# A delta-rule layer's forward substitution moved from GpSimd to VectorE, with the inverses' scratch in its two tiles

## The chip, the cores and the metric

The kernel runs on one core of one Trainium2 chip. The metric is the device time of one execution in microseconds (us). One core has five engines with an instruction queue each: TensorE (PE in the profile; its weight loads are PEld), VectorE (DVE), ScalarE (ACT), GpSimd (POOL) and SyncE (SP), which here issues most transfers between HBM and the on-chip buffer SBUF. Each engine works through its own list in order; an instruction that needs another engine's or a transfer's result waits for a semaphore, and everything behind it on its engine waits with it.

## What is computed

The reference is a decoder trunk of four pre-norm residual layers over 256 tokens and 1024 channels: a pooling mixer, a gated delta-rule mixer, a latent-attention mixer, and a pooling mixer again. The change touches only the second layer. Its core, cut to what matters, is:

```python
L = where(strict, einsum('bhnid,bhnjd->bhnij', k_beta, k) * decay, 0)
A = eye(C) + L                       # C = 64 tokens a chunk, 8 heads, 4 chunks
sol = triangular_solve(A, concat([v_beta, k_beta * exp(g)]), lower=True)
```

So a lower triangular matrix with ones on its diagonal has to be inverted for each head and chunk. The kernel takes the 256 tokens as two tiles of 128, one matrix of 128x128 for each tile and head (16 in all), in place of chunks of 64.

## The kernel before

All products of activations with weights run in three passes on TensorE: a float32 weight block is split into a high part (`whi`, ScalarE, L117) and a rest (`wlo`, L119, mostly on VectorE, in named cases on GpSimd), and `mm3` (L126 to L129) or `rows` (L167) adds up the three partial products. `weights` (L104 to L124) loads 512 KB from HBM on SyncE's queue into a tile `raw`, then makes the two parts of each 128x512 block. A block feeds 12 matmuls of 256 columns or 6 of 512 columns, so TensorE needs a fresh `wlo` from VectorE about every 1.4 us. The tiles `raw`, `whi`, `wlo` go round in rings.

The delta-rule layer (`gdn_layer`) runs through this list: `g0 k0 d a0 g1 k1 a1 s q0 v0 i v1 v2 q1 g2 u0 v3 u1 g3`. Here g are gate projections, k keys, q queries, v values (each a projection of 512 columns, for k, q and v followed by a short convolution on VectorE, L636, and a SiLU on ScalarE, L777 for values), a the lower triangles `LT`, d the decays, s the substitution, i the inverses, u first products with the inverses. The list is only the order in which the program is traced. The order in which each engine meets its instructions is set afterwards by a scheduler, which plays the program through with assumed durations and gives each engine what is ready first; so an edit in one place can shift rows of every engine near it. `issue_after` (the helper `later`) adds an order on one engine only: what is traced inside it comes behind the named instruction if that stands on the same engine.

The part that is changed works as follows.

- `substitution` (L713 to L744). The four 32x32 blocks on the diagonal of each of the 16 matrices, 64 blocks in all, are brought through HBM into a tile `Lb` with one block on each of 64 partitions (eight transfers `d_l<-LT`, L718, and one `Lb<-d_l`, L721). `Tb`, in the same layout, begins as 64 unit matrices. For r = 0 to 30 one instruction multiplies column r of the block with row r of the inverse so far, as an outer product of 31-r rows and r+1 columns, into `pr` (L726), and a second subtracts it from the rows of `Tb` below (L730). These 62 instructions depend on each other one by one. Then `Tb` goes to HBM (`d_t<-Tb`, L733) and comes back in eight transfers into the tiles `T` (L737). All of L726 and L730 runs on GpSimd.
- `mark["blocks"]` is the last of those instructions. The GpSimd work of `queries` (L758 to L763, with the power at L657) is put behind it.
- `inverses` (L788 to L840). VectorE transposes `T` into `U` (L800); TensorE multiplies `T` with `LT` (L809), VectorE masks the result into a scratch tile `X1` (L811), of which GpSimd has set one part to zero (L799), TensorE goes on with `X1` and `U` (L815), VectorE subtracts (L818), and a second round (L823 to L836) joins blocks of 64 to the full inverse. This is done for each of the two token tiles.

## Time and profile before

| quantity | value |
|---|---|
| runs of the kernel before | 859.46 us median of 3 (859.01 to 860.44) |
| the profiled execution, its own time | 857.47 us |
| its span in the trace | 855.8 us |
| mean granted TensorE clock | 0.991 |
| TensorE busy | 835.1 us, 98% of the span |
| VectorE busy | 594.5 us, 69% |
| ScalarE busy | 489.7 us, 57% |
| GpSimd busy | 153.7 us, 18% |

The profiled execution is one run; its time is 1.7 us longer than its span, and 2.0 us under the median of the timed runs. In the profile a row of a group gives the line, engine and operation, the tile written and the tiles read, the shape, how many there were, busy time and mean length, and the idle time ahead of them with what ended it. A row of a timeline gives the start, the length of the merged piece, and in brackets the idle time before it. Instructions that follow each other on one engine overlap a little in these rows: the next one starts before the last one's length is over. A row of the windows view gives, for each stretch, the busy time and count on each engine, the granted TensorE clock as a share of full speed, the share of the DMA engines in use and the GB/s moved. Line numbers are those of the kernel before.

### The profile page before, as it was taken

To read this page: it belongs to the slowest core of one execution; us is meant where nothing else is said; L and a number is where in the kernel's file an instruction comes from. 1 tells how busy PE (TensorE), PEld (TensorE's weight loads), DVE (VectorE), ACT (ScalarE), POOL (GpSimd) and SP (SyncE) were. 2 spreads that over 40 slices of the span, in tenths; PEclk is the share of its full clock that TensorE was granted. 3 is DMA by queue.
4 is the path that set the end of the run, shared out by engine and by line. 5 is a ranking of instruction groups with operands and counts; after the bars stand their busy time and mean duration, and the time that the engine had idled before them with its cause. 6 is when DMAs were issued, how large, how long until landed. Compare 5 with 4: busy or idle time off the path is not lost.

```text
span 855.8 us, 16129 instructions
## 1 busy us (share of the span) xinstructions
PE 835.1 (98%) x5967; PEld 777.7 (91%) x5967; DVE 594.5 (69%) x1140; ACT 489.7 (57%) x1007; POOL 153.7 (18%) x290
## 2 busy tenths in 40 slices
PE   7999999999999979999999999999999999999996
PEld 6999998988999969888979998999989989999986
DVE  4579876566988967556567659778767568766852
ACT  5565655467845635555465654566555576555642
POOL 5000000234227952032202002000000210000012
PEclk9999999999999989999999999999999999999998
DMA  6756656646655552222557676743652547666551
GB/s 201 250 177 194 179 191 210 184 148 203 191 146 156 169 172 90 85 74 99 172 154 215 204 157 174 195 137 93 171 167 75 173 151 217 178 192 182 194 195 51
DMA packets 111288, 140.43 MB, mean 164 GB/s; under 512 B 23340, under 2 KB 53224, under 8 KB 111208
## 3 DMA queue, kind: packets, MB, share of 16 engines
q1 hardware_dynamic: 109056, 138.17, 53.7%
q0 software_dynamic: 320, 1.06, 0.4%
q8 instruction: 47, 0.77, 0.4%
q10 hardware_dynamic: 1832, 0.16, 0.2%
q14 instruction: 33, 0.27, 0.1%
HBM read 137.79 MB, written 1.58 MB: 163 GB/s over the span
## 4 chain that ended last, share of the span: by engine, by line
PE 86%; DVE 4%; POOL 3%; issue 2%; DMA 2%; ACT 1%; SPq 1%; POOLq 0%; ACTq 0%
PE acc L167 34%; PE acc L128 12%; PE acc L127 12%; PE acc L129 12%; PE aux L127 2%; PE aux L128 2%; PE aux L129 2%; DVE vc L636 1%; DVE wlo L119 1%; DMA raw<-in_pool_w_in_dram 1%; PE aux L688 1%; DVE h L303 1%; PE aux L809 1%; PE tp L1168 1%; ACT junk L209 1%
## 5 line engine op out<-in xcount | busy, mean ns | idle before, releaser
L119 DVE TENSOR_TENSOR wlo<-raw,whi 128x512 fp32r<-128x512 f32 (+1 forms) x493 | 343.3, 719 | 161.9 <-ACT whi L117 159.9
L117 ACT CAST whi<-raw 128x512 fp32r<-128x512 f32 (+1 forms) x508 | 302.0, 619 | 263.1 <-PE acc L167 90.0
L128 PE MATMUL acc<-hTl,whi 128*128 128x256 f32 x832 | 235.5, 283 | 0.0
L127 PE MATMUL acc<-hTh,whi 128*128 128x256 f32 x832 | 234.5, 282 | 0.0
L129 PE MATMUL acc<-hTh,wlo 128*128 128x256 f32 x832 | 234.4, 282 | 0.0
L128 PEld LDWEIGHTS acc<-hTl,whi 128*128 128x128 f32 x832 | 157.3, 189 | 0.5
L127 PEld LDWEIGHTS acc<-hTh,whi 128*128 128x128 f32 x832 | 157.2, 189 | 0.5
L129 PEld LDWEIGHTS acc<-hTh,wlo 128*128 128x128 f32 x832 | 157.2, 189 | 0.2
L167 PE MATMUL acc<-whi,yTh 128*128 128x256 f32 (+1 forms) x384 | 116.2, 323 | 0.0
L167 PE MATMUL acc<-wlo,yTh 128*128 128x256 f32 (+1 forms) x384 | 116.2, 319 | 0.0
L167 PE MATMUL acc<-whi,yTl 128*128 128x256 f32 (+1 forms) x384 | 92.4, 321 | 0.0
L167 PEld LDWEIGHTS acc<-wlo,yTh 128*128 128x128 f32 x384 | 72.0, 188 | 5.1
L167 PEld LDWEIGHTS acc<-whi,yTh 128*128 128x128 f32 x384 | 71.8, 188 | 5.2
L167 PEld LDWEIGHTS acc<-whi,yTl 128*128 128x128 f32 x384 | 63.0, 188 | 5.6
L291 POOL TENSOR_TENSOR hg<-x,gain 128x256 f32<-128x256 f32 x18 | 15.3, 858 | 258.2 <-DVE x L353 255.5
L167 PE MATMUL acc<-whi,hTh 128*128 128x512 f32 (+1 forms) x144 | 55.8, 395 | 1.1 <-ACT hTh L195 1.0
L167 PE MATMUL acc<-wlo,hTh 128*128 128x512 f32 (+1 forms) x144 | 56.2, 396 | 0.4 <-DVE wlo L119 0.2
L167 PE MATMUL acc<-whi,hTl 128*128 128x512 f32 (+1 forms) x144 | 45.8, 390 | 0.0
L434 POOL COPY win<-u 128x4 f32<-128x4 f32 x8 | 2.8, 355 | 178.1 <-ACT u L428 178.1
L167 PEld LDWEIGHTS acc<-whi,hTh 128*128 128x128 f32 x144 | 27.4, 190 | 7.8 <-ACT hTh L195 2.2
L167 PEld LDWEIGHTS acc<-wlo,hTh 128*128 128x128 f32 x144 | 27.5, 191 | 6.8 <-DVE wlo L119 1.7
L167 PEld LDWEIGHTS acc<-whi,hTl 128*128 128x128 f32 x144 | 26.9, 190 | 5.8 <-DVE hTl L200 0.4
(337 smaller groups left out, 1437.0 us busy)
## 6 DMA issues: line engine op xcount, KB each, us to landing
raw<-in_pool_w_in_dram SPq DMA_DIRECT2D x60, 512.0 KB, 4.4
raw<-in_gdn_w_in_dram SPq DMA_DIRECT2D x48, 512.0 KB, 4.1
raw<-in_pool_w_out_dram SPq DMA_DIRECT2D x32, 512.0 KB, 4.4
raw<-in_mla_w_in_dram SPq DMA_DIRECT2D x24, 512.0 KB, 4.2
raw<-in_mla_w_uq_dram SPq DMA_DIRECT2D x36, 256.0 KB, 3.8
raw<-in_pool_w_grp_dram SPq DMA_DIRECT2D x16, 512.0 KB, 3.9
raw<-in_gdn_w_out_dram SPq DMA_DIRECT2D x16, 512.0 KB, 3.6
raw<-in_mla_w_ukv_dram SPq DMA_DIRECT2D x32, 256.0 KB, 3.4
```

The source lines that it names most:

```text
L117: a = nc.scalar.copy(hi, v)
L119: b = e.tensor_tensor(out=lo, in0=v, in1=hi.bitcast(F32), op=ALU.subtract)
L127: nc.tensor.matmul(o, lhsT=lhs[0], rhs=rhs[0], start=start, stop=False)
L128: nc.tensor.matmul(o, lhsT=lhs[0], rhs=rhs[1], start=False, stop=False)
L129: nc.tensor.matmul(o, lhsT=lhs[1], rhs=rhs[0], start=False, stop=stop)
L167: nc.tensor.matmul(o, lhsT=act(k, t * P, P)[x], rhs=parts[j][z][:, sl], start=k == first and x == z == 0, stop=k == last and x == 1)
L209: nc.scalar.activation(junk[:, :n], src, AF.Square, scale=scale, accum_out=o)
L291: nc.gpsimd.tensor_tensor(out=self.early[t, a], in0=xs[t][:, sl], in1=self.g[:, sl], op=ALU.mult)
L303: nc.vector.scalar_tensor_tensor(out=h[:, cut:], in0=xs[t][:, sl], scalar=r[:, 0:1], in1=self.g[:, sl], op0=ALU.mult, op1=ALU.mult)
L636: nc.vector.scalar_tensor_tensor(out=o[:, d:], in0=ps[:, :S - d], scalar=tp(3 - d, c), in1=o[:, d:], op0=ALU.mult, op1=ALU.add)
L688: nc.tensor.matmul(ps[:, b], lhsT=kT[hf][:, b, tt], rhs=rhs[hf][:, b, tt], start=True, stop=True)
L809: nc.tensor.matmul(ps[:, h], lhsT=LT[t][:, h], rhs=blocks(T[t], 0)[:, h], start=True, stop=True)
```

## The change

The two instructions of the substitution's loop are issued on VectorE in place of GpSimd. The scratch tiles `X1` of the inverses are no longer allocated; the full-height tiles that hold `Lb` and `Tb` are kept in a list, and `X1[0]` and `X1[1]` are views of them (32x32 elements a partition seen as 8x128). `Lb` and `Tb` themselves are, as before, the first 64 partitions. Nothing of the arithmetic changes.

```diff
-        Tb = big("Tb", B, B)[:M * Q]
+        Tb_ = big("Tb", B, B)
+        Tb = Tb_[:M * Q]
+        free = []
         nc.gpsimd.memset(Tb, 0.0)
         nc.gpsimd.memset(Tb.rearrange("m r c -> m (r c)")[:, ::B + 1], 1.0)
...
-            Lb = big("Lb", B, B)[:M * Q]
+            Lb_ = big("Lb", B, B)
+            Lb = Lb_[:M * Q]
+            free.extend((Lb_, Tb_))
             nc.sync.dma_start(out=Lb, in_=d_l.rearrange("m (r c) -> m r c", r=B))
             pr = small("pr", 256, bufs=1)[:M * Q]
             for r in range(B - 1):
                 n, c = B - 1 - r, r + 1
                 pv = pr[:, :n * c].rearrange("m (a b) -> m a b", a=n)
-                nc.gpsimd.tensor_tensor(out=pv, op=ALU.mult,
+                nc.vector.tensor_tensor(out=pv, op=ALU.mult,
                                         in0=Lb[:, r, r + 1:, None].to_broadcast([M * Q, n, c]),
                                         in1=Tb[:, r:r + 1, :c].to_broadcast([M * Q, n, c]))
                 tv = Tb[:, r + 1:, :c]
-                mark["blocks"] = nc.gpsimd.tensor_tensor(out=tv, in0=tv, in1=pv,
+                mark["blocks"] = nc.vector.tensor_tensor(out=tv, in0=tv, in1=pv,
                                                          op=ALU.subtract).ins
...
             U.extend(big("U", H, P) for _ in range(NT))
-            X1 = [big("X1", H, P) for _ in range(NT)]
+
+            X1 = [a.rearrange("p (h a) c -> p h (a c)", h=H) for a in free]
             for t in range(NT):
                 nc.gpsimd.memset(X1[t][:, :, 32:64], 0.0)
```

The edit moves line numbers by 2 to 5: the substitution's pair L726 and L730 becomes L730 and L734, `T` with `LT` L809 becomes L814, the transposes of the values L781 become L785, the scratch's zeros L799 become L804.

The scheduler's order of the engines changes with it. On VectorE, at the place where the substitution's input has landed, before (the projections' `wlo`, the query's `attnT`, the values' convolution `vc`):

```order
L119 TENSOR_TENSOR wlo<-raw,whi 128x512 x2
L679 TENSOR_REDUCE ssq<-sq 128x2x2
L119 TENSOR_TENSOR wlo<-raw,whi 128x512
L692 SCALAR_TENSOR_TENSOR attnT<-aux,rk,DT 128x128 x7
L679 TENSOR_REDUCE ssq<-sq 128x2x2
L692 SCALAR_TENSOR_TENSOR attnT<-aux,rk,DT 128x128
L636 SCALAR_TENSOR_TENSOR vc<-acc,tap,vc 128x255 x2
L119 TENSOR_TENSOR wlo<-raw,whi 128x512 x2
```

And now at the same place:

```order
L119 TENSOR_TENSOR wlo<-raw,whi 128x512
L730 TENSOR_TENSOR pr<-Lb,Tb 64x31
L734 TENSOR_TENSOR Tb<-Tb,pr 64x31
L730 TENSOR_TENSOR pr<-Lb,Tb 64x60
L734 TENSOR_TENSOR Tb<-Tb,pr 64x30x2
L730 TENSOR_TENSOR pr<-Lb,Tb 64x87
L681 TENSOR_REDUCE ssq<-sq 128x2x2
L734 TENSOR_TENSOR Tb<-Tb,pr 64x29x3
L730 TENSOR_TENSOR pr<-Lb,Tb 64x112
L694 SCALAR_TENSOR_TENSOR attnT<-aux,rk,DT 128x128 x2
```

From here to the last subtraction the 62 instructions of the substitution lie on VectorE among 82 others: 30 of L119, 42 of the convolution L636, 8 of `attnT` and 2 reductions. 25 of the 62 are followed directly by the next of the substitution, 37 by something else.

On TensorE, at the first product that reads `T`, before (numbers tell the tiles of a ring apart; `acc_4263` and `acc_4264` are the two banks of the last value projection, v3):

```order
L127 MATMUL acc_4263<-hTh0_2258,whi_4272 128x256
L128 MATMUL acc_4263<-hTl0_2259,whi_4272 128x256
L129 MATMUL acc_4263<-hTh0_2258,wlo_4271 128x256
L127 MATMUL acc_4263<-hTh0_2258,whi_4272 128x256
L809 MATMUL aux_3509<-T_2517,LT_2531 128x64 x8
L128 MATMUL acc_4263<-hTl0_2259,whi_4272 128x256
L129 MATMUL acc_4263<-hTh0_2258,wlo_4271 128x256
```

And now (the same projection's banks are `acc_4261` and `acc_4262`, its last block is `wlo_4371`):

```order
L127 MATMUL acc_4261<-hTh1_2267,whi_4372 128x256
L128 MATMUL acc_4261<-hTl1_2268,whi_4372 128x256
L129 MATMUL acc_4261<-hTh1_2267,wlo_4371 128x256
L814 MATMUL aux_3507<-T_2517,LT_2531 128x64 x8
L785 MATMUL tp_3931<-ident_101,vc_3921 128x128 x4
L785 MATMUL tp_3948<-ident_101,vc_3938 128x128 x4
L820 MATMUL aux_3517<-U_3501,Lb_3045 96x64 x8
L814 MATMUL aux_3527<-T_2518,LT_2532 128x64 x8
L677 MATMUL tp_4118<-ident_101,kqT_4093 128x128 x4
L127 MATMUL acc_4262<-hTh0_2258,whi_4266 128x256
```

The product has moved down. Between the last query product `attnT` of q0 and the first product with `T`, TensorE had 275 matmuls of 256 columns and 48 of 512 columns before, and now has 314 and 48; the transposes between them (L781, now L785) are 16 in both.

On GpSimd the 62 instructions are gone, the work of `queries` (L758 to L763) for the first four heads moves ahead of the place where the substitution ends, since its order behind `mark["blocks"]` binds only one engine, and the two memsets of the scratch (L799, now L804) come behind it, for they now wait until `Lb` and `Tb` have been read for the last time. On SyncE 18 weight loads instead of 15 stand between `Lb<-d_l` and `d_t<-Tb`, and none stands between `d_t<-Tb` and `T<-d_t`.

## The prediction

> **What bounds the kernel now.** I read the first part of the page, then TensorE's waits in the delta-rule layer (200 to 420 us), then the chain of waits and the windows around the longest of them.
>
> ```profile
> PE 835.1 (98%) x5967; PEld 777.7 (91%) x5967; DVE 594.5 (69%) x1140; ACT 489.7 (57%) x1007; POOL 153.7 (18%) x290
> ```
>
> ```profile
> PE aux L809 <- DMA T<-d_t: 6.1, 1, 6.1
> PE tp L675 <- ACT kqT L669: 0.9, 1, 0.9
> PE tp L781 <- ACT vc L777: 0.8, 1, 0.8
> ```
>
> TensorE is busy for 98% of the span, so the time ends where TensorE's work ends, and it moves only by what TensorE waits or is slowed. Its one long wait in this layer is for `T`, the result of the substitution. The chain of waits shows what that wait consists of (start, length, what):
>
> ```profile
> 306.45 0.59 POOL Tb L730
> ...
> 307.06 2.93 DMA d_t<-Tb
> ...
> 310.93 1.95 DMA T<-d_t
> ...
> 313.01 3.65 PE aux L809 x16
> ...
> 322.40 1.79 PE aux L809 x16
> ```
>
> The last subtraction ends at 307.06, and the way through HBM takes 5.95 us more until L809 starts at 313.01. The same 16 matmuls take 3.65 us there and 1.79 us for the second tile. The windows say why, and how full VectorE is meanwhile (columns: sum, PE, PEld, DVE, ACT, POOL, granted clock, DMA share, GB/s):
>
> ```profile
> 260.00:270.00 10.00, 10.00 (x87) 10.00 (x86) 8.41 (x21) 6.11 (x13) 8.70 (x17) 1.00 0.41 133
> 270.00:280.00 10.00, 9.22 (x77) 8.82 (x77) 10.00 (x20) 6.15 (x12) 9.14 (x12) 1.00 0.55 160
> 280.00:290.00 10.00, 10.00 (x87) 9.97 (x87) 10.00 (x18) 7.24 (x16) 9.21 (x13) 1.00 0.58 159
> 290.00:300.00 10.00, 9.93 (x58) 8.35 (x57) 8.41 (x15) 4.78 (x10) 9.22 (x13) 1.00 0.54 159
> 300.00:310.00 10.00, 6.88 (x38) 5.71 (x36) 6.95 (x10) 3.43 (x6) 9.13 (x15) 1.00 0.51 138
> ...
> 312.00:313.00 1.00, 0.00 (x0) 0.02 (x1) 0.00 (x0) 0.81 (x2) 0.00 (x0) 0.50 0.41 66
> 318.00:319.00 1.00, 1.00 (x9) 1.00 (x8) 0.21 (x2) 0.62 (x1) 0.00 (x0) 0.75 0.71 219
> ```
>
> After the wait the granted clock is 0.50 until some way into 318. That costs 3.65 - 1.79 = 1.9 us on L809 and, by the nine matmuls after it that follow at 0.21 instead of 0.12 us in the chain, about 0.9 more: 2.8 us. And VectorE, not GpSimd alone, is nearly full just here: 43.8 of the 50 us from 260 to 310. That is the engine the work moves to.
>
> **What the move takes off VectorE.** The splits `wlo` of VectorE are longer while GpSimd computes; first the groups from 100 to 250 us, then from 255 to 308:
>
> ```profile
> L119 DVE TENSOR_TENSOR wlo<-raw,whi 128x512 fp32r<-128x512 f32 x86 | 59.5, 713 | 30.4 <-ACT whi L117 30.0 <-PE acc L128 0.2
> ```
>
> ```profile
> L119 DVE TENSOR_TENSOR wlo<-raw,whi 128x512 fp32r<-128x512 f32 x29 | 27.2, 949 | 7.6 <-ACT whi L117 7.6
> ```
>
> So 29 x (0.949 - 0.713) = 6.8 us of VectorE's time there is waiting behind GpSimd, and it goes. GpSimd keeps these in the stretch (its groups, 255 to 312; in the new order they come ahead of the substitution's end):
>
> ```profile
> L119 POOL TENSOR_TENSOR wlo<-raw,whi 128x512 fp32r<-128x512 f32 x2 | 2.6, 1292 | 0.0
> L657 POOL TENSOR_TENSOR rq<-rq,halves 128x8 f32<-128x8 f32 x1 | 2.0, 1968 | 0.1
> L758 POOL TENSOR_TENSOR Gb<-Gb,kqT 128x512 f32<-128x512 f32 x1 | 1.3, 1257 | 0.0
> L759 POOL TENSOR_SCALAR rq<-ssq 128x8 f32<-128x8 f32 x1 | 0.5, 526 | 0.1
> ```
>
> That is 6.4 us of GpSimd. Before, 6.8 us of delay came with some 45 us of it, 0.15 us per us; the substitution's own instructions, which also read two tiles from SBUF, can now be delayed too, so I take 1.0 us (bounds 0 and 6.4). The Trainium skill, page "SBUF — State Buffer", section "SBUF: two separate sides", is stricter: GpSimd and a VectorE instruction with two SBUF inputs share one port pair, and whoever comes second waits for the other's whole instruction. The rows agree that only `wlo` suffers, and the convolution, which has one input in PSUM, does not. By that rule at its full strength the term would be 6.4 us in place of 1.0.
>
> **What it puts on VectorE.** No row shows the two instructions on VectorE. The nearest are tensor_tensor on SBUF tiles at both ends of their size (31 to 256 elements a partition), then one pair in which the second needs the first:
>
> ```profile
> L439 DVE TENSOR_TENSOR win<-win,corr 128x60 f32<-128x60 f32 x2 | 0.4, 208 | 0.0
> L435 DVE TENSOR_TENSOR win<-u 128x1020 f32<-128x1020 f32 x8 | 9.7, 1217 | 1.0 <-ACT u L428 1.0
> L967 DVE SCALAR_TENSOR_TENSOR rr<-kf,rr 128x64 f32<-128x64 f32 x4 | 0.9, 220 | 0.0
> ```
>
> ```profile
> 83.15 0.48 DVE L967 SCALAR_TENSOR_TENSOR rr<-kf,rr 128x64 f32<-128x64 f32 x2
> ```
>
> From 60 to 1020 elements the length grows by 1.051 ns an element, from a base of 208 - 60 x 1.051 = 145 ns. Each of the two instructions handles (31-r)(r+1) elements at step r, 5,456 over the 31 steps. So the 62 are 62 x 0.145 + 10,912 x 0.001051 = 20.5 us long. The pair takes 0.48 where each is 0.22, so a dependent successor costs 0.04 us on top. An independent one overlaps: in the timeline rows below, two L119 of 0.68 take 1.29, so one takes 0.61 of the engine's time. In the new order 25 of the 62 are followed by their own successor and 37 by something else, which at 0.08 us overlap gives 20.5 + 25 x 0.04 - 37 x 0.08 = 18.5 us. All overlapped it would be 15.5, none 23.0; the order decides for 18.5.
>
> What lies among them is priced by these rows of VectorE's timeline:
>
> ```profile
> 258.05 1.29 DVE L119 TENSOR_TENSOR wlo<-raw,whi 128x512 fp32r<-128x512 f32 x2 [2.35 <-ACT whi L117]
> 262.48 1.89 DVE L692 SCALAR_TENSOR_TENSOR attnT<-aux,rk,DT 128x128 f32<-128x128 f32 x7
> 264.30 0.68 DVE L679 TENSOR_REDUCE ssq<-sq 128x4 f32<-128x512 f32 x1
> 264.89 0.34 DVE L692 SCALAR_TENSOR_TENSOR attnT<-aux,rk,DT 128x128 f32<-128x128 f32 x1
> 290.76 2.03 DVE L636 SCALAR_TENSOR_TENSOR vc<-acc,tap,vc 128x253 f32<-128x253 f32 x5
> ```
>
> 30 splits at 0.61 are 18.3 us; 42 of the convolution at (2.03 - 0.47)/4 = 0.39, where 0.47 is one alone, 16.4; 8 `attnT` at (1.89 - 0.34)/6 = 0.26, 2.1; 2 reductions at 264.89 - 264.30 = 0.59, 1.2. Together 38.0 us. The windows bound it from below: 43.8 us busy from 260 to 310, less the 6.8, are 37.0.
>
> **The sum.** The substitution starts when `Lb` lands, which doesn't move; on GpSimd that was here:
>
> ```profile
> 259.39 0.23 POOL L726 TENSOR_TENSOR pr<-Lb,Tb 64x31 f32<-64x31 f32 x1 [13.50 <-DMA Lb<-d_l]
> ```
>
> On VectorE it then ends at 259.4 + 38.0 + 18.5 + 1.0 = 316.9, if VectorE waits for nothing else. ScalarE's `whi` and the weight loads, for which it waited 7.6 us before, are now ahead, since VectorE is the slow one. The way through HBM is unchanged, 5.95 us, so `T` reaches TensorE at 322.85 instead of 313.01: 9.8 us later. Against this stands what TensorE has done by then. The order puts 314 matmuls of 256 columns ahead of the first product with `T` instead of 275, and their price is in TensorE's timeline (132 steps lie between the first two rows):
>
> ```profile
> 259.55 0.37 PE L129 MATMUL acc<-hTh,wlo 128*128 128x256 f32 x1
> ...
> 275.26 0.28 PE L129 MATMUL acc<-hTh,wlo 128*128 128x256 f32 x1
> 276.32 0.66 PE L781 MATMUL tp<-ident,vc 128*128 128x128 f32 x4 [0.78 <-ACT vc L777]
> ```
>
> That is 0.119 us each, 4.6 us for 39, which TensorE no longer has to do afterwards. Net: 9.8 - 4.6 = 5.2 us slower.
>
> Has TensorE work until then? Up to the first transposes of the values (276.32) the convolutions set the pace in both orders; now only 95 projection matmuls lie ahead of them, 38 fewer, and TensorE waits some 5 us there. From there to L809 it took 30.6 us (to 306.88); 77 more matmuls make it 39.8, and with about 1.2 us for the second pair of transposes it arrives at 317.3. It waits 5.5 us for `T`, about as long as before, so I leave the 2.8 us of half clock in place. After `T`, 48 matmuls of v3 remain as filling that need no new split, instead of 80; I count nothing for that, and it would cost up to 3 us if the steps from X1 to the full inverse show between them.
>
> At nothing I put the shared scratch. Its zeros (L799) now wait for the last read of `Lb` and of `Tb` by `d_t`, which is over some 3 us before `T` is back; behind these zeros on GpSimd stands only the second heads' work for outputs past 355 us. If that cover were gone, the price is two memsets, 0.6 us. On SyncE no weight load stands between `d_t` and `T` any more; the loads ahead of `d_t` wait for splits that come before the substitution's end. VectorE's transposes of `T` (L800) hold what is queued behind them for some 6 us, as they did for 4.0; TensorE's next splits are made by then.
>
> The profiled execution took 857.47 us, so the sum is 862.7; it lies 2.0 under the median of the runs, for which the forecast is 859.46 + 5.2 = 864.7 us. A difference of 0.2% (1.7 us) is about what a measurement of this kernel can tell from none.
>
> **The rivals.**
> - *VectorE has room* (faster). If the 62 overlap throughout (15.5), the rest is at its lower bound (37.0) and GpSimd holds nothing, the substitution ends at 311.9 and `T` is there at 317.85, just as TensorE arrives. Then there is no wait, the clock stays up, and the start at 317.3 to 317.85 gives 4.3 - 4.6 - 2.8 = about -3 us: 856.4. It decides by whether the substitution ends before 312. For it speaks the 6.8 us that come free; against it that the windows show 10.00 of 10 from 270 to 290, where no gap is to be filled. Chance 0.14.
> - *A wash*. The same bounds, but TensorE still waits long enough for half clock: 317.85 - 313.01 - 4.6 = +0.2, 859.7; half the GpSimd and overlap terms with a warm clock come out within 1.7 us as well. Chance 0.16.
> - *GpSimd still holds VectorE* (much slower). The 6.4 us of GpSimd's remaining work delay the two-input instructions one for one: +5.4 on the forecast, +10.6, 870.1. For it speaks that the substitution itself now reads two SBUF tiles at every step; against it the 0.15 us per us seen so far. The skill's rule named above would give this. Chance 0.14.
> - The forecast, +5.2 with its own range from +2 to +9: 0.56.
>
> So slower by over 0.2% has 0.56 + 0.14 = 0.70, within 0.2% 0.16, faster 0.14. The range goes from 857.5, which leaves out most of the faster case, to 870.5.
>
> **What would show it.** In the changed profile: L119 on VectorE near 0.72 us between 260 and 316; L734's last near 316 to 317, in place of L730's 306.45; VectorE at 9.5 or more of 10 from 262 to 316; L814's first start near 323 with a wait of 4 to 7 us for `T<-d_t`; a wait of some 5 us of L785 on the values' SiLU near 271 to 276. The prediction is wrong if the last L734 ends before 312, if VectorE shows gaps of more than 5 us in all while the substitution runs, or if TensorE's time after `T` changes by more than the 4.6 us.

## The result, and the profile after

The changed kernel takes 873.44 us (median of 4 runs, 870.73 to 875.10), the kernel before 859.32 us beside it (4 runs). The ratio is 1.0159 with a 95% interval of 1.0132 to 1.0186: 14.1 us slower. The forecast was 5.2 us slower, with a range from 857.5 to 870.5 us, so the direction is right, the size is not, and the time lies outside the range. The profiled execution took 870.73 us, its span 869.0, 13.2 more than the span before.

TensorE's waits in the delta-rule layer come first, again from 200 to 420 us (what waited, for what, us in total, times, longest):

```profile
PE acc L127 <- DVE vc L636: 7.4, 1, 7.4
PE aux L814 <- DMA T<-d_t: 6.2, 1, 6.2
PE acc L127 <- DVE cv L636: 1.4, 1, 1.4
```

The wait for `T` is as long as it was (6.1), but it is no longer alone. A second one of 7.4 us is new: a projection waits for a PSUM bank that the values' convolution on VectorE has not yet read out. The chain of waits shows where `T` is:

```profile
320.94 0.19 DVE Tb L734
...
321.15 2.87 DMA d_t<-Tb
...
324.47 2.17 DMA T<-d_t
...
326.69 3.46 PE aux L814 x15
```

The last subtraction ends at 321.13, not at 316.9, the way through HBM is 5.56 us, and `T` is used at 326.69 instead of 313.01, 13.7 us later. The windows of the same stretch show both waits and what each costs in clock (columns as in the prediction):

```profile
260.00:270.00 10.00, 8.77 (x75) 8.57 (x73) 9.83 (x30) 4.42 (x10) 4.54 (x5) 1.00 0.36 109
270.00:280.00 10.00, 3.86 (x18) 3.89 (x19) 10.00 (x27) 4.37 (x9) 0.00 (x0) 0.59 0.46 154
280.00:290.00 10.00, 10.00 (x79) 10.00 (x79) 9.43 (x24) 6.16 (x12) 0.00 (x0) 0.89 0.35 100
...
310.00:320.00 10.00, 10.00 (x67) 9.08 (x66) 7.68 (x20) 5.59 (x12) 0.00 (x0) 1.00 0.63 204
320.00:330.00 10.00, 3.76 (x20) 3.56 (x20) 2.87 (x7) 0.00 (x0) 0.62 (x2) 0.65 0.30 58
330.00:340.00 10.00, 9.84 (x80) 9.62 (x79) 6.12 (x12) 6.09 (x15) 1.28 (x1) 0.83 0.01 2
```

VectorE is busy for 9.4 to 10 of 10 us up to 310, as forecast, and then for 7.7 of 10, which was not forecast. TensorE is idle twice, and after each wait its granted clock is about half for several us.

That gives a ledger of TensorE's time: what it idles, and what it loses to the lower clock. One window over the layer, 200 to 380 us, of before, of after, and (for later) of one experiment each, held_v3 and dense_24:

```profile
200.00:380.00 180.00, 172.03 (x1224) 158.95 (x1223) 135.11 (x279) 104.63 (x217) 78.30 (x112) 0.98 0.47 141
```
```profile
200.00:380.00 180.00, 164.36 (x1171) 152.54 (x1169) 139.17 (x324) 98.31 (x200) 37.43 (x41) 0.94 0.45 136
```
```profile
200.00:380.00 180.00, 169.67 (x1215) 157.09 (x1214) 145.49 (x338) 102.93 (x216) 38.47 (x48) 0.97 0.46 138
```
```profile
200.00:380.00 180.00, 173.92 (x1237) 159.78 (x1236) 138.62 (x299) 105.31 (x219) 69.98 (x96) 0.99 0.47 142
```

Idle is 180 less the second number: 8.0 us before, 15.6 after. For the clock I cut the stretch into 36 windows of 5 us and sum busy time x (1 - granted clock): 2.4 us before, 6.4 after. Together 10.4 and 22.0, so 11.6 of the 13.2 us are TensorE's idleness and its clock in this layer. Seen from TensorE the loss is the new early wait and the half clock behind it, since the wait for `T` has not grown. That is the same loss as the 13.7 us by which `T` is later, looked at from the other side, and the two are not to be added up.

### The profile page after: what moved, and what is told of

Same layout as the page of the kernel before. It is cut to its first block, busy times and chain, and to the rows that moved or that the text cites. A ratio compares the mean times of both kernels' runs of the same rounds, so it can differ in the third digit from the quotient of the medians.

```text
span 869.0 us, 16137 instructions
## 1 busy us (share of the span) xinstructions
PE 839.1 (97%) x5967; PEld 780.7 (90%) x5967; DVE 605.6 (70%) x1202; ACT 489.1 (56%) x1007; POOL 114.5 (13%) x228
## 4 chain that ended last, share of the span: by engine, by line
PE 87%; DVE 5%; DMA 3%; POOL 2%; ACT 1%; issue 1%; SPq 0%; POOLq 0%; ACTq 0%; DVEq 0%
PE acc L167 33%; PE acc L127 13%; PE acc L128 13%; PE acc L129 13%; PE aux L127 2%; PE aux L128 2%; PE aux L129 2%; DVE wlo L119 1%; PE aux L690 1%; DVE h L303 1%; DMA gain<-in_norm_g_dram 1%; PE tp L1173 1%; DMA raw<-in_gdn_w_in_dram 1%; PE tp L323 1%; DMA raw<-in_pool_w_in_dram 1%
## 5 line engine op out<-in xcount | busy, mean ns | idle before, releaser
L119 DVE TENSOR_TENSOR wlo<-raw,whi 128x512 fp32r<-128x512 f32 (+1 forms) x493 | 333.7, 699 | 150.3 <-ACT whi L117 145.4
L119 POOL TENSOR_TENSOR wlo<-raw,whi 128x512 fp32r<-128x512 f32 x15 | 20.4, 1363 | 76.3 <-ACT whi L117 48.6
```

The lines of the kernel that those rows point to most:

```text
L119: b = e.tensor_tensor(out=lo, in0=v, in1=hi.bitcast(F32), op=ALU.subtract)
```

## The experiments

Eighteen kernels and the theories that they were to tell apart:

- **V**: VectorE is full, the 62 instructions lengthen its work one for one, and `T` is late by that. In a sharper form **Q**: each step waits for its turn, so `T` comes when all that the order puts ahead of the last subtraction on its engine is done, and the chain's own length matters little. **L**, against Q: the chain itself is slow on VectorE.
- **S**: the shared scratch holds the inverses.
- **O**: the loss is the new order, first thought of as TensorE's, later as the place that the steps have among the splits.
- **H**: GpSimd holds VectorE. **W**: what is lost is TensorE's wait for a late `T`. **D**: VectorE has time for the steps, but not by the moment at which TensorE needs `T`.

**The two parts of the change, one at a time.** First only the scratch (L730 and L734 back on GpSimd):

```diff
-                nc.vector.tensor_tensor(out=pv, op=ALU.mult,
+                nc.gpsimd.tensor_tensor(out=pv, op=ALU.mult,
```

> The shared scratch alone: the substitution stays on GpSimd, X1 is a view of the tiles of Lb and Tb. Theory V (VectorE is full in this stage, and the 62 instructions lengthen its work there one for one, so T comes late): within 1.5 us of before, 858 to 861. Rival S (the scratch's zeros, now behind the last read of Lb and Tb, hold the inverses): a good part of the 14 us, 863 or more. Rival O (the loss is the scheduler's new order of TensorE): as before, since TensorE has the same 275 and 48 matmuls ahead of T as before.

Measured: 859.73 us (10 runs, 857.56 to 862.24), ratio 0.9998 (0.9983 to 1.0013). Then only the move, the inverses' scratch in tiles of its own:

```diff
-            X1 = [a.rearrange("p (h a) c -> p h (a c)", h=H) for a in free]
+            X1 = [big("X1", H, P) for _ in range(NT)]
```

> The move alone: the substitution on VectorE, X1 in tiles of its own. Theory V: as the whole change, 871 to 875, and the last subtraction near 321. Rival S: 860 to 867. Rival O: as the whole change too, since TensorE has 314 and 48 matmuls ahead of T as in the whole change.

Measured: 872.68 us (870.08 to 875.04), ratio 1.0142 (1.0111 to 1.0172). The scratch costs nothing, S falls, and the move is the whole loss.

**More of the same, and half of it.** The changed kernel with each multiplication issued twice:

> The whole change with each of the 31 multiplications issued twice in a row (the second writes the same numbers to pr). That is 31 x 0.145 + 5,456 x 0.00105 = 10.2 us more in length, some 8 to 10 us of VectorE's time. TensorE's order ahead of T stays at 314 and 48 matmuls. Theory V: the last subtraction and the time move by that amount, 881 to 884. Rival O: VectorE's extra time falls into waits that the order makes anyway, less than 3 us, below 876.5.

Measured: 883.49 us (881.88 to 884.45), ratio 1.0266 (1.0246 to 1.0286). TensorE's waits:

```profile
PE aux L817 <- DMA T<-d_t: 18.7, 1, 18.7
PE acc L127 <- DVE vc L636: 7.5, 1, 7.5
```

The wait for `T` grows from 6.2 to 18.7 us, the early one stays. Then the kernel before with steps 16 to 30 on VectorE (16 for N):

```diff
-                nc.gpsimd.tensor_tensor(out=pv, op=ALU.mult,
+                eng = nc.gpsimd if r < N else nc.vector
+                eng.tensor_tensor(out=pv, op=ALU.mult,
```

> The kernel before with steps 0 to 15 of the substitution on GpSimd and steps 16 to 30 on VectorE (X1 in tiles of its own, the queries' GpSimd work behind step 15). GpSimd took 25 us for these steps; on VectorE they are 30 x 0.145 + 5,200 x 0.00105 = 9.8 us, and VectorE had some 8 us free between 290 and 310 and gets some 3 us back from splits that no longer wait. Theory V: the last subtraction near 300 to 303, TensorE's wait for T of 6.1 us mostly gone, 851 to 857. Rival O: TensorE's order changes here more than in the whole change (355 and 96 matmuls ahead of T), so it is slower than before by 5 us or more.

Measured: 867.67 us (866.33 to 868.94), ratio 1.0084 (1.0065 to 1.0103). V's time is missed by more than 10 us. The tile's instructions by engine, and one of TensorE's waits and one of its windows behind `T`:

```profile
L731 POOL TENSOR_TENSOR Tb<-Tb,pr x16: 266/608/1072, 258.4 to 279.9; 64x31 f32<-64x31 f32 x1, 64x60 f32<-64x60 f32 x1, 64x87 f32<-64x87 f32 x1, 64x112 f32<-64x112 f32 x1
L731 DVE TENSOR_TENSOR Tb<-Tb,pr x15: 183/356/1251, 284.4 to 319.4; 64x255 f32<-64x255 f32 x1, 64x252 f32<-64x252 f32 x1, 64x247 f32<-64x247 f32 x1, 64x240 f32<-64x240 f32 x1
```
```profile
PE aux L817 <- DVE X L813: 4.4, 1, 4.4
```
```profile
350.00:360.00 10.00, 9.33 (x60) 8.52 (x59) 4.51 (x10) 1.84 (x3) 0.00 (x0) 0.50 0.00 0
```

GpSimd is done with its half at 280 (first and last start are the two numbers after the durations). VectorE, at some 0.36 us an instruction, needs until 319 for the other half, because 23 splits and 28 pieces of convolution stand among its 30 instructions. So the place in the queue, and not the amount of work, decides when the chain ends: theory Q. The time is another matter. O in its first form said 5 us slower or more, because the order puts more of TensorE's work ahead of `T`, and it is hit (7.7): 451 projection matmuls stand between the last query product and `T`, instead of 323, and TensorE has no wait for `T` on its list. Behind `T` no projection of the values is left to fill its waits; it waits 4.4 us for VectorE's mask and runs at half clock. The ledger is 9.6 idle + 12.7 clock.

**Place or chain.** The changed kernel with the splits of the third and fourth block of values (v2, v3) made to wait for the last subtraction, so that none stands among the steps (`mark["last"]` is that subtraction):

```diff
         def values(vi):
+            kept = held_back["after"]
+            if vi in (2, 3):
+                held_back["after"] = [mark["last"]]
...
+            held_back["after"] = kept
             vR.append(big("vR", NT, CW))
```

> The changed kernel, but the splits of the third and fourth block of values are put behind the last subtraction, so that VectorE's order holds, from the first multiplication to the last subtraction, the 62 instructions among 24 pieces of convolution, 8 attnT and 2 reductions and no split at all (in the changed kernel 30 splits and 42 pieces). Theory Q (the place in the queue: T comes when everything that the order puts ahead of the last subtraction on its engine is done): 259.7 + 18.5 to 23.0 + 24 x 0.39 + 8 x 0.26 + 2 x 0.59, so the last subtraction ends at 291 to 296 instead of 321.1. Theory L (the chain itself is slow on VectorE, because each instruction needs the one before): the steps stay as far apart as they were and it ends near 315 or later. The time is not the point: 338 projection matmuls instead of 586 stand ahead of T, so TensorE has some 29 us of work left for afterwards; with T 25 to 28 us sooner and TensorE short of splits meanwhile both theories allow 868 to 890.

Measured: 875.65 us (874.55 to 878.59), ratio 1.0192 (1.0173 to 1.0211). The tile's subtractions, and TensorE's waits:

```profile
L734 DVE TENSOR_TENSOR Tb<-Tb,pr x31: 183/349/418, 260.6 to 294.3; 64x31 f32<-64x31 f32 x2, 64x60 f32<-64x60 f32 x2, 64x87 f32<-64x87 f32 x2, 64x112 f32<-64x112 f32 x2
```
```profile
PE acc L129 <- DVE wlo L119: 14.7, 1, 14.7
PE tp L789 <- ACT vc L785: 8.1, 3, 4.0
```

The same 62 instructions are over at 294.5 instead of 321.1: Q holds, L falls. But the time is no better. What waited for `T` now waits for splits.

**Fewer splits on VectorE.** The changed kernel with four more splits of v1 and v2 each, and of the queries' projections, on GpSimd; by its order 8 fewer lie among the steps:

```diff
-                            pool=() if which else (0, 4))
+                            pool=(1, 3, 5, 7) if which else (0, 4))
...
-                            pool=((1, 3, 5, 7), (), (), ())[vi])
+                            pool=((1, 3, 5, 7), (1, 3, 5, 7), (1, 3, 5, 7), ())[vi])
```

> The changed kernel with 8 splits taken off VectorE within the substitution (22 of them stand among its instructions instead of 30) and given to GpSimd, which has nothing else to do there. Theory Q: 8 x 0.61 = 4.9 us less ahead of the last subtraction, so it ends near 316.2 instead of 321.1, and the time goes to about 869 (867 to 871). Rival H (GpSimd holds VectorE for its whole instruction whenever both read two tiles): 8 splits of GpSimd of about 1.5 us cost VectorE up to 1.1 each, 8.8 us, against the 4.9: last subtraction near 325, time near 877.

Measured: 879.72 us (878.74 to 880.31), ratio 1.0233 (1.0219 to 1.0247). The groups from 255 to 335 us, of after and of this kernel:

```profile
L119 DVE TENSOR_TENSOR wlo<-raw,whi 128x512 fp32r<-128x512 f32 x33 | 22.1, 680 | 4.7 <-ACT whi L117 4.6
...
L730 DVE TENSOR_TENSOR pr<-Lb,Tb 64x31 f32<-64x31 f32 (+15 forms) x31 | 11.1, 359 | 1.2 <-DMA Lb<-d_l 0.8
L734 DVE TENSOR_TENSOR Tb<-Tb,pr 64x31 f32<-64x31 f32 (+15 forms) x31 | 11.0, 354 | 0.4
```
```profile
L730 DVE TENSOR_TENSOR pr<-Lb,Tb 64x31 f32<-64x31 f32 (+15 forms) x31 | 14.7, 475 | 3.8 <-DMA Lb<-d_l 3.3
L734 DVE TENSOR_TENSOR Tb<-Tb,pr 64x31 f32<-64x31 f32 (+15 forms) x31 | 11.2, 362 | 0.5
...
L119 POOL TENSOR_TENSOR wlo<-raw,whi 128x512 fp32r<-128x512 f32 x11 | 17.8, 1622 | 26.4 <-ACT whi L117 15.2 <-PE acc L129 11.1
```

The steps take 25.9 us instead of 22.1, nearly all of it in the multiplications, and the first one starts 1.3 us later. With that the 4.9 us that the 8 splits should have freed are gone: the last subtraction starts at 321.9 instead of 320.9. H's time is nearly hit (877), its size is not: 3.8 us on the steps for nine more GpSimd splits of 1.62, some 0.26 us per us and not one for one. The rest of this kernel's loss is in the ledger: 18.3 idle + 11.0 clock, 7.2 more than in the changed kernel, and 4.6 of it are clock. Why the clock stays low for longer behind `T` was not tried. The Trainium skill, page "Perfetto Trace Analysis", section "Optimizing Scalar/DVE Operations", warns that GpSimd and VectorE share an SBUF read port, so that shifting work between the two might not help. This run agrees, with the numbers above.

**Work as such, or its due time.** A floor, with the 62 instructions left out:

> A floor: the changed kernel with the 62 instructions of the substitution left out altogether, so T holds unit blocks and the output is another one. Neither VectorE nor GpSimd has the work, and T is there early. From the kernel before: 6.1 us of wait for T and 2.8 us of half clock go, so about 850.5 (847 to 853). It serves as the base for the next kernel.

Measured: 849.01 us (848.32 to 849.27), ratio 0.9875 (0.9858 to 0.9892). All that the substitution costs is 10.7 us before and 24 after. Then the 62 on VectorE with a result that nobody reads:

```diff
+            Td = big("Td", B, B)[:M * Q]
+            nc.gpsimd.memset(Td, 0.0)
...
-                                        in1=Tb[:, r:r + 1, :c].to_broadcast([M * Q, n, c]))
-                tv = Tb[:, r + 1:, :c]
+                                        in1=Td[:, r:r + 1, :c].to_broadcast([M * Q, n, c]))
+                tv = Td[:, r + 1:, :c]
```

> The floor kernel with the same 62 dependent instructions on VectorE again, but on a tile whose result nobody reads: T still holds unit blocks and is there early (so the output is another one). Its distance to the floor is what the instructions cost as work in VectorE's full order, without any wait for T. Theory V (VectorE is full, its 18.5 us have to be paid wherever they stand): most of it is lost, 7 to 14 us over the floor, since TensorE then waits for splits and convolutions instead. Rival W (what is lost is TensorE's wait for a late T): within 3 us of the floor.

Measured: 873.72 us (872.58 to 874.25), ratio 1.0163 (1.0142 to 1.0183). This looked like proof of V, but its trace says otherwise (waits of all engines, 320 to 350 us):

```profile
POOL Lb L806 <- DVE pr L732: 12.1, 1, 12.1
PEld aux L822 <- POOL Lb L806: 6.0, 1, 6.0
PE aux L822 <- issue: 5.8, 1, 5.8
```

The steps still read `Lb`, the scratch lies in `Lb`, and its zeros wait for the last step. The inverses waited for the chain after all, through the shared tile, so this run tells nothing. The same with scratch tiles of its own and `T` filled from `Lb`:

```diff
-            nc.sync.dma_start(out=d_t.rearrange("m (r c) -> m r c", r=B), in_=Tb)
+            nc.sync.dma_start(out=d_t.rearrange("m (r c) -> m r c", r=B), in_=Lb)
```

> The changed kernel with scratch tiles of its own for the inverses and with T filled from Lb instead of from the substitution's result (so T is there near 266 and the output is another one); the 62 dependent instructions stay on VectorE and nobody waits for them but a few late GpSimd instructions. This mends the earlier idle chain, whose end held the inverses through the shared Lb tile. Floor: 849.0. Theory V (VectorE's time has to be paid wherever the steps stand): 7 to 14 us over the floor, 856 to 863, with TensorE waiting for splits and convolutions. Rival W (what is lost is TensorE's wait for a late T): at most 852.

Measured: 853.33 us (850.43 to 855.52), ratio 0.9941 (0.9922 to 0.9959). And on the kernel before, all steps on GpSimd:

> The same on the kernel before: all 62 instructions on GpSimd, T filled from Lb, so that nobody waits for them. Both theories: only the longer splits on VectorE are left (6.8 us of VectorE's time by the trace of before), so 849 to 855; what the kernel before has above that is its wait for T.

Measured: 852.98 us (852.68 to 856.20), ratio 0.9937 (0.9917 to 0.9957). Both lie some 5 us over the floor by their ratios (0.9941 - 0.9875 = 0.0066, 5.7 us; 5.3 for GpSimd). The idle chain on VectorE, in one window over 260 to 350 us, first the changed kernel, then this one:

```profile
260.00:350.00 90.00, 76.23 (x545) 72.49 (x544) 75.12 (x175) 43.55 (x90) 13.29 (x15) 0.89 0.43 128
```
```profile
260.00:350.00 90.00, 87.58 (x664) 81.06 (x662) 85.89 (x197) 51.43 (x104) 13.39 (x15) 1.00 0.49 148
```

VectorE does the steps and 10.8 us more work in the same 90 us, TensorE 119 matmuls more at full clock. It can, because the last step may come at 346. The time lies between the two forecasts (856 to 863 and at most 852), so V as stated falls and W is not met either: the work costs about 5 us, in the order that the scheduler gives to these kernels, and the rest of the 24 is owed to when `T` is due.

**An order between the two.** D says that no order does both in time, O that a better one does. The changed kernel with only the splits of v3 held behind the last subtraction (the same edit with `vi in (3,)`); 21 splits instead of 30 then lie among the steps:

> The changed kernel, all 31 steps on VectorE, with only the splits of the fourth block of values put behind the last subtraction: 21 splits instead of 30 lie among the steps, the 42 pieces of convolution stay. Theory D (a due date: VectorE can do the steps and its other work by about 345, but not by the 307 at which TensorE needs T): the list is 18.5 + 21 x 0.61 + 42 x 0.39 + 3.3 = 51 us, last subtraction near 311 to 314; T some 7 to 10 us sooner than in the changed kernel, 4 to 7 later than before; time 864 to 871, still slower than before. Rival O (the loss is only the place that the order gave the steps): such an order brings it back to 860.

Measured: 860.85 us (12 runs, 859.82 to 863.24), ratio 1.0020 (1.0009 to 1.0030). O is right and D is not. 12.6 of the 14.1 us come back by nine splits that stand elsewhere. Its subtractions and waits:

```profile
L734 DVE TENSOR_TENSOR Tb<-Tb,pr x31: 182/351/417, 260.8 to 313.1; 64x31 f32<-64x31 f32 x2, 64x60 f32<-64x60 f32 x2, 64x87 f32<-64x87 f32 x2, 64x112 f32<-64x112 f32 x2
```
```profile
PE acc L129 <- DVE wlo L119: 8.9, 1, 8.9
PE tp L789 <- ACT vc L785: 0.7, 1, 0.7
```

The last subtraction ends at 313.3, where D put it, 7.8 us sooner than in the changed kernel, though 6.3 later than before. The early wait of 7.4 us is not there: the order puts 157 projection matmuls between the last query product and the first transposes of the values, instead of 95 (before: 133), and 189 from there to `T`, instead of 267 (before: 190). `T` is no longer waited for; one long wait is left, 8.9 us for the splits that were held back, and one stretch of low clock. The ledger is 10.3 idle + 2.8 = 13.1, 2.7 over before; the span is 2.9 over.

Is the hold a gain by itself? The same hold in the kernel before, all steps on GpSimd, whose TensorE order stays 133 and 190:

> The kernel before, all steps on GpSimd and the two splits left there, with only the splits of the fourth block of values put behind the last subtraction. In the changed kernel this one edit brought 12.6 of 14.1 us back. If the held splits are a gain by themselves, the ratio is 0.993 to 0.997 here too; if they only undo what the move did to VectorE's order (theory O), VectorE has no steps to be freed for and the ratio is 0.999 to 1.003.

Measured: 859.62 us (12 runs, 856.84 to 860.77), ratio 0.9989 (0.9976 to 1.0002). It is not: it only undoes what the move did to VectorE's queue.

**Toward a version that beats both.** GpSimd's order before has two splits of 1.29 us between the steps. With these on VectorE:

```diff
-                            pool=((0, 4), (7,), (3, 7), (7,))[vi])
+                            pool=((0, 4), (7,), (), (7,))[vi])
```

> The kernel before, substitution on GpSimd, with the two splits that stand in GpSimd's order between the substitution's steps (1.29 us each) given to VectorE. Theory Q: the last subtraction ends 2.6 us sooner, near 304.5, T is there near 310.4, and the time falls by 2 to 3 us: ratio about 0.997. If VectorE's two more splits or TensorE's arrival (some 10 matmuls fewer ahead of T) take it back, the ratio is 1.000. Theory L says nothing else here.

Measured: 863.44 us (862.30 to 864.45), ratio 1.0044 (1.0031 to 1.0056): slower, against Q. The multiplications on GpSimd, 255 to 312 us, before and here:

```profile
L726 POOL TENSOR_TENSOR pr<-Lb,Tb 64x31 f32<-64x31 f32 (+15 forms) x31 | 18.1, 584 | 15.6 <-DMA Lb<-d_l 13.5
```
```profile
L726 POOL TENSOR_TENSOR pr<-Lb,Tb 64x31 f32<-64x31 f32 (+15 forms) x31 | 21.1, 680 | 15.6 <-DMA Lb<-d_l 13.3
```

They got 3.0 us longer while VectorE was fuller (9.99 of 10 us from 290 to 300 instead of 8.41), and the subtractions 0.4 shorter, so the 2.6 us were given back: the last subtraction ends at 307.4. TensorE waits 9.7 us for `T` with a changed order (142 and 175). But 3.5 of the 6.1 us between the spans come far behind this stage, as the end of this section shows. The same two splits moved, the last 7 steps on VectorE (N = 24) and v3's splits held:

> The kernel before with the same two splits on VectorE and only the last 7 of the 31 steps on VectorE; the splits of the fourth block of values stand behind the last subtraction, so that only 3 splits and 7 pieces of convolution lie among these 14 instructions. Theory Q: GpSimd's 24 steps end near 296.3, VectorE's list is 14 instructions of 4.4 us in all, 3 x 0.61 and 7 x 0.39, so the last subtraction ends near 305 if VectorE is not behind when they begin; time near 857.5, ratio 0.996 to 0.999. Theory L (chain slow on VectorE as such): it ends after 307 and the ratio is above 1.000.

Measured: 855.50 us (854.38 to 856.68), ratio 0.9952 (0.9940 to 0.9965), the fastest of the kernels that leave nothing out. TensorE's waits:

```profile
PE acc L167 <- DVE vc L636: 4.3, 2, 3.4
PE aux L816 <- ACT vR L791: 1.1, 1, 1.1
```

The last subtraction ends at 305.8, 1.2 us sooner than before, and there is no wait for `T`. The ledger is 6.1 idle + 1.6 = 7.7, against 10.4. Four kernels take parts of it away. First the 7 steps: all of them on GpSimd, with the two splits on VectorE and v3's splits held:

> The mixed kernel that beat the kernel before (last 7 steps on VectorE, the splits of the fourth block of values behind the last subtraction, ratio 0.9952), with all 31 steps left on GpSimd: only the order of the splits is changed. If the held splits alone make the gain, the ratio is again near 0.995. If the 7 steps on VectorE are needed too, the last subtraction comes at 305 to 307 and the ratio is 0.998 to 1.003.

Measured: 862.19 us (11 runs, 860.64 to 864.71), ratio 1.0030 (1.0018 to 1.0042); the last subtraction ends at 307.5. Then v3's splits not held, with the 7 steps and the two splits on VectorE:

> The mixed kernel with the last 7 steps on VectorE, but without holding the splits of the fourth block of values: 8 splits and 7 pieces of convolution then lie among the 14 instructions instead of 3 and 7. Theory Q (place in the queue): 5 x 0.61 = 3 us later than with the held splits, last subtraction near 309, ratio 0.999 to 1.004. If moving the 7 steps alone makes the gain, the ratio is near 0.995.

Measured: 856.57 us (12 runs, 854.19 to 860.50), ratio 0.9968 (0.9955 to 0.9982). The last subtraction is as late as Q said (309.9, which is 2.8 us later than before), and the kernel is faster all the same, against Q: TensorE has 344 projection matmuls ahead of `T`, instead of 323, and waits only 2.3 us for it. The last 5 steps instead of 7:

> The mixed kernel that beat both, with only the last 5 of the steps on VectorE: 10 instructions with 1 split and 6 pieces of convolution among them. Theory D: GpSimd's 26 steps end some 2.5 us later than its 24 did, VectorE's list is 3 us shorter, so the last subtraction is at 305 to 306 as with 7 steps, and the ratio 0.994 to 0.998. If VectorE's steps themselves bring the gain, fewer of them bring less: 0.998 or more.

Measured: 858.51 us (11 runs, 856.54 to 859.74), ratio 0.9976 (0.9966 to 0.9987), with the last subtraction at 307.4 and not at 305 to 306. And the 7 steps with the held splits, but the two GpSimd splits left where they were:

> The same with the last 7 steps on VectorE, so that only one split (and 12 pieces of convolution) stands among these 14 instructions, and GpSimd keeps its splits. Theory O: the last subtraction at about 306 (GpSimd 1.3 us later by its one split, VectorE's list 2 x 0.61 - 5 x 0.39 = about the same) and the ratio 0.995 to 0.999.

Measured: 858.30 us (12 runs, 857.06 to 861.53), ratio 0.9984 (0.9971 to 0.9997). The last subtraction ends at 307.0.

By the times alone, the 7 steps gain only together with the two splits. With these on VectorE, 1.0044 becomes 0.9968 and, v3 held, 1.0030 becomes 0.9952; with these on GpSimd and v3 held, 0.9989 becomes 0.9984, which is no difference. The 7 steps with neither of the other two edits were not run. The traces show that the times mix two places. In all these kernels TensorE has 3,472 or 3,473 matmuls left from the first of the inverses' products with the values on (`aux<-vR,U`, some 40 us behind `T`). From its start to the end of the span it is 500.8 to 500.9 us in the kernel before, scratch_only, held_v3, hold_plain, dense_24, late_24_own and dense_26, but 503.2 in the changed kernel, 504.4 in own_queue and hold_only, and 505.4 in dense_24_plain. In these last three the extra time comes almost whole between 660 and 710 us, where the third layer passes into the fourth; there the orders of TensorE, VectorE and ScalarE are not those of before, while in the other kernels with 500.8 to 500.9 they are the same, instruction by instruction. The same 20 us, before and in dense_24_plain:

```profile
680.00:700.00 20.00, 19.61 (x126) 17.10 (x125) 12.77 (x24) 13.18 (x28) 4.92 (x10) 1.00 0.38 121
```
```profile
680.00:700.00 20.00, 18.25 (x99) 15.10 (x98) 12.45 (x23) 13.33 (x29) 5.51 (x10) 0.91 0.44 132
```

Up to that product the 7 steps gain in each pairing: it starts at 351.2 instead of 357.7 (dense_24_plain against hold_plain), at 352.9 instead of 356.5 (dense_24 against hold_only) and at 355.4 instead of 357.5 (late_24_own against own_queue). These are one profiled execution each, and such an execution can lie 2 to 3 us from its kernel's median (the changed kernel's 2.7 below it). So in their own stage the 7 steps at the end, where VectorE had room before (8.41 and 6.95 of 10 from 290 to 310), make the gain, and a reordering some 300 us behind them takes it back in dense_24_plain and makes most of own_queue's and hold_only's loss. What makes the scheduler reorder there was not tried. By the times the held splits add 1 us or nothing: the intervals of 0.9952 and 0.9968 overlap.

## Why the prediction was wrong

Between the forecast (5.2 us slower) and the measurement (14.1) lie 8.9 us. `T` came 13.7 us later and not 9.8: 3.9. The 4.6 us that TensorE was to save behind `T` shrank to 0.5: 4.1. The last 0.9 lie between the profiled executions (13.2) and the medians. So two terms of the sum failed, by about as much: the end of the substitution, and the credit for matmuls done ahead of `T`.

- **What goes off VectorE**: right. L119 takes 680 ns from 255 to 335, instead of the 949 before (255 to 308); 720 was forecast.
- **What comes on**: right. With GpSimd nearly idle beside it, in dense_all, the two instructions are 10.4 + 10.3 = 20.7 us long; 20.5 was worked out.
- **GpSimd's 1.0 us**: right in size. Two steps that met a GpSimd split (1.75 us from 297.10, 1.53 us from 302.77) took 1.11 and 1.10 us instead of 0.40 and 0.39, 1.4 us in all. The rival that gave 870.1 came closest by its number, not by its mechanism.
- **The end of the substitution at 316.9, "if VectorE waits for nothing else"**: this step failed. VectorE's timeline, and one row of ScalarE's:

```profile
259.66 0.40 DVE L730 TENSOR_TENSOR pr<-Lb,Tb 64x31 f32<-64x31 f32 x1 [0.79 <-DMA Lb<-d_l]
...
298.02 1.11 DVE L734 TENSOR_TENSOR Tb<-Tb,pr 64x252 f32<-64x252 f32 x1
303.46 1.10 DVE L730 TENSOR_TENSOR pr<-Lb,Tb 64x240 f32<-64x240 f32 x1
315.45 0.69 DVE L119 TENSOR_TENSOR wlo<-raw,whi 128x512 fp32r<-128x512 f32 x1 [1.21 <-ACT whi L117]
318.14 0.69 DVE L119 TENSOR_TENSOR wlo<-raw,whi 128x512 fp32r<-128x512 f32 x1 [0.97 <-ACT whi L117]
```
```profile
317.49 0.62 ACT L117 CAST whi<-raw 128x512 fp32r<-128x512 f32 x1 [1.60 <-DMA raw<-in_gdn_w_in_dram]
```

  VectorE waits for `whi` after all, 2.8 us in four places (the two longest, near its end, are shown), and each time the next steps stand behind the split. ScalarE in turn had waited for the weights themselves. "ScalarE's `whi` and the weight loads are now ahead" had it backwards: a load needs a slot that a split frees, the splits were late behind the steps, and so the loads were late too. SyncE's queue fits this; from 255 to 330 us its weight loads wait for VectorE's steps and splits:

```profile
SPq L104 <- DVE Tb L734: 23.6, 4, 11.3
SPq L104 <- DVE wlo L119: 15.9, 6, 9.1
```

  With the start 0.3 us later and the two holds of 1.4 (1.0 was counted) these make up 3.5 of the 4.2 us between 316.9 and 321.13. The way through HBM was 0.4 us shorter than before.
- **The 4.6 us for 39 matmuls done earlier**: this step failed too. From the first product with `T` to the end of the span it is 542.8 us before and 542.3 after, so 0.5 us was saved. The 39 were counted from the last query product on; ahead of `T` in all stand only 32 more (1,392 of these matmuls instead of 1,360), as the prediction's own 48 left instead of 80 says. At 0.119 us that is 3.8. From the first product with `T` to the first of the inverses' products with the values it is 42.0 us before and 39.2 after, 2.8 less:

```profile
354.92 3.19 PE L850 MATMUL aux<-vR,U 128*128 128x256 f32 x14
```
```profile
365.84 3.75 PE L855 MATMUL aux<-vR,U 128*128 128x256 f32 x16
```

  So 10.9 us of loss stand at this place. Another 2.3 come in the rest of the program, with the same 3,472 matmuls: 1.0 within 60 us behind this product, the rest between 660 and 710 us, where the scheduler's order is another one (see above). The sum put nothing on the layers behind.
- **The early wait of about 5 us near 271 to 276, and the half clock left "in place"**: the wait was seen (it is 7.4 us, for a PSUM bank and not for the SiLU), its own half clock was not: the clock is 0.50 from 272 to 282, and the clock's loss in the layer is 6.4 us, not 2.4. In a sum that goes by when `T` comes this costs nothing by itself, since the order fixes what TensorE does ahead of `T`, and it still stood there 6.2 us early. Behind `T` the half clock was rightly left in place (3.3 us of loss up to the product above, 2.7 before).
- **The three signs of being wrong**: none of them came. The last subtraction ended after 312, VectorE's gaps were 2.8 us and not over 5, and TensorE's time after `T` changed by 0.5. The third was no sign at all, since a change of 0 there already takes the whole credit away.
- **The scratch at nothing**: right, 0.9998. That it is cheap hangs on the chain's end, as idle_chain shows.
- **The order was taken as given.** It was read rightly, 30 splits among the steps, and the sum made from it. Whether those splits had to stand there wasn't asked, and that is where 12.6 of the 14.1 us are.

What stays open: held_v3 changes VectorE's order and with it TensorE's (95 matmuls become 157), and which of the two removes the early wait was not tried apart. It also loses nothing in the later layers, so some 2.3 us of what it brings back lie behind the substitution's stage. Why the order of the later layers changes is open too.

## What to carry to other kernels

Before moving a serial chain to a faster engine, count what the order will put between its steps, not how much faster each step is: here a multiplication takes 359 ns on VectorE instead of 584, and the chain is over 14 us later. Moving only its tail, where the target engine has room (together with two splits and some held back), turned 1.6% slower into 0.5% faster; with the whole chain moved, keeping back work that its result does not need turned it into 0.2% slower. When a scheduler sets the order, compare the whole program and not only the stage that was edited: three of these kernels lost 3.5 to 4.5 us in layers that no edit touched. Price every wait of the bound engine together with the lower clock behind it, and check that a run meant to remove a dependence has not kept it through a shared buffer.

## What the runs showed of the hardware

- The holding between GpSimd and VectorE goes both ways: GpSimd's multiplications grow from 584 to 680 ns when VectorE is fuller (own_queue), VectorE's from 359 to 475 when GpSimd has nine more splits (relief_q). In own_queue the same GpSimd multiplication of 64x135 took 1.43 us at 262.76, with VectorE busy, and 0.41 at 303.38, with VectorE idle. On average the loss is a fraction of the other's time (0.26 us per us in relief_q), while single instructions lose 0.7 us at once (1.11 instead of 0.40).
- The Trainium skill, page "GPSIMD Engine Reference", section "4.1 Engine selection", puts elementwise two-input work on VectorE, GpSimd being about half as fast. For the single instruction the traces agree (354 against 721 ns for the subtraction in its place); for the kernel's time, what stood ahead in the queue outweighed it.
